# A decoder layer's kernel: the modulations ask for their weights one row of k tiles per portion, and VectorE makes one low part in two of the output projection's pairs

## The chip, the cores and the metric

The kernel runs on one core of one Trainium2 chip. The metric is the device time of one execution in microseconds (us). A core has TensorE (matmuls), VectorE, ScalarE and GpSimd (elementwise work), SyncE (here only issuing DMAs), and 16 DMA engines that all queues share. In the profile they are called PE, PEld (TensorE's weight loads), DVE, ACT, POOL and SP.

## What is computed

One layer of a decoder for 512 prompt tokens and 8 x 8 sample tokens, 576 columns in all, with D = 1024, in float32. Cut to what matters here:

```python
mod = jax.nn.silu(c) @ w_ada + b_ada          # 6 blocks of 1024, per sequence
sh1, sc1, g1, sh2, sc2, g2 = jnp.split(mod, 6, axis=-1)
h = _rmsnorm(x, norm1_g) * (1.0 + sc1) + sh1
b_gate, c_gate, xa, q, k, v, ga, gb = jnp.split(h @ w_in, cuts, axis=-1)
uc, new_conv = _causal_conv(c_gate * xa, conv_buf, conv_w)
ya = (b_gate * uc) @ w_conv_out
yb = attend(q, k, v, sinks) @ w_attn_out
x = x + g1 * ((jax.nn.sigmoid(ga) * ya + jax.nn.sigmoid(gb) * yb) @ w_mix_out)
h2 = _rmsnorm(x, norm2_g) * (1.0 + sc2) + sh2
# then the ConvFFN with w_up, w_down, its residual with g2, and a final RMSNorm
```

## The kernel before

**Products in three passes.** Every float32 operand is split into a high part (a copy to the matmul's type, made by ScalarE) and a low part (the operand minus the high part). A product is high x high + high x low + low x high, for each of the 8 tiles of 128 rows of k. Each operand needs its two parts before its matmuls.

**Pairs.** Most products are made two at a time (`pair_product`, line 382). Seven products of half the columns (288) replace eight: parts 1 to 7, of 12 matmuls each, with four sums of the weights ("A" holds a0 and a1, "B" holds s1 and b1, "C" holds s2 and s4, "D" holds s3) and sums of the operand. The four PSUM banks are X and W (from the pool `aux`, four banks) and Y and Z (from the pool `mm`, two tiles, so each pair takes over the banks of the pair before). Part 2 fills Y with s2, part 3 fills Z with s1. VectorE reads Y after part 2 (`u`, seen as `uv<-mm,p`); part 6 goes on in Y; VectorE reads it again after part 6 (`v`, the same form), and Z after part 7 (`uv<-mm,uv`). Only then can the next pair's parts 2 and 3 begin.

**The weights of a pair** are prepared during the pair before (`pair_weights`, line 326) from two raw tiles ra and rb of 128 x 8 x 128. `in_turn` (line 377) hangs the steps behind the parts: before part 1 "sums1 ah al", after part 2 "dh dl sums2", after part 3 "bh bl", after part 4 "ch cl". `sums1` and `sums2` are VectorE's sums, in place: `sums1` overwrites rb and makes the raw of "D", `sums2` overwrites ra (`raw<-raw,raw` and `raw<-raw` in the profile). A step with h is ScalarE's high part, one with l the low part. A low part is made in one of two ways:

```python
if name in adding:
    act.activation(lo, src, AF.Copy, scale=-1.0)
    pool.dma_start(lo, src, accum_op=ALU.add)
else:
    dve.tensor_tensor(out=lo, in0=src, in1=hi.bitcast(F32), op=ALU.subtract)
```

In the first way the transfer issued by GpSimd adds the raw weights, read from ra, to the negated copy. `al` reads ra, `sums2` writes it, so `sums2` waits for that transfer. The call's string names the weights that go the first way.

**Stages.** After the start-up, the keys, queries and values, and the convolution's products, come: four pairs for the gate B (`b_pair`), eight pairs for ga and gb (`sigmoid_pair`, "gate pairs"), two products and three pairs with `w_conv_out` (`out_pair`, lines 1424 to 1469; the projection's pairs), eight products with `w_attn_out` (lines 1497 to 1521), the products with `w_mix_out`, and the FFN. The weights of the first out pair are prepared in the last gate pair with `OUT_ADDING`; those of the second and third in the out pair before each (line 1459).

**The modulations as filler.** Two thirds of `mod` are made in between, by generators that run in portions: each step of a product over one k tile calls `tick()` (line 204), which adds a rate to a counter and runs a portion whenever it passes 1. A pair has 28 ticks, a product 8. `modulation(2048)` follows the attention's portions at `MOD_RATE`, during the B and gate pairs; `modulation(4096)` runs at the rate of line 1475 during the eight products with `w_attn_out`; what is left is run off by `drain()` behind them. One call makes 16 blocks of 128: for each k tile four loads of 128 x 512 of `w_ada` ("a row", tiles `ada`), a group of 16 small matmuls per two k tiles (`side_by_side`, line 1166, seen at L1171), then ScalarE copies the PSUM bank (`row`), TensorE transposes it (four transposes) and VectorE adds the bias.

**Queues and tiles.** TensorE, ScalarE and VectorE keep program order for what goes through the wrappers `pe`, `act` and `dve` (from line 1298 on); the row copy on ScalarE and the bias sum on VectorE do not go through them and are placed by the compiler's scheduler. SyncE's loads are placed by the scheduler too until line 1474, from where they keep program order. Tiles such as `ada`, `th`, `uv`, `mxh` and `st` share one pool of 57; a new one waits for the release of an old one. During the products with `w_attn_out` SyncE also loads, behind the fifth product, the state of the FFN (`st`, six tiles) and the residual x.

Of the kernel before, what the change touches and what calls it, by code (L numbers as in the profile page):

```python
# [30 lines left out]
CACHE_AT = 15, 16  # L31
UP_ADDING, FIRST_TICKS = "BD", 12
ATT_RATE, ADDING_FROM, B_PAIRS = 0.285, 3, ((0, 4), (1, 5), (2, 6), (3, 7))
B_ADDING, OUT_ADDING, MOD_RATE = "BD", "BCD", 12 / 190
EPS = 1e-6
NEG = -1e33
A_BUFS = 57
# [37 lines left out]
def step_kernel(ctx: ExitStack, tc: tile.TileContext, ins: dict, outs: list):  # L75
# [15 lines left out]
    def nm(s):  # L91
        cnt[0] += 1
        return f"{s}{cnt[0]}"

    def slot(s, dt=F32, shape=None):
        return ap_.tile(shape or [P, NT], dt, tag="a", name=nm(s))
# [4 lines left out]
    def aux():  # L101
        return pa.tile([P, 512], F32, tag="aux", name=nm("aux"))
# [49 lines left out]
    def load_w(src, nk):  # L152

        raw = wp.tile([P, nk, P], F32, tag="raw", name=nm("raw"), bufs=W_BUFS)
        sync.dma_start(raw, src)
        return raw
# [42 lines left out]
    def fill(gen, rate):  # L199
        filler[:] = [gen, rate, 0.0]  # L200
# [125 lines left out]
    def pair_weights(ra, rb, adding=""):  # L326


        c0, c1 = slice(0, 4), slice(4, 8)
        w = {}  # L330

        def add(out, x, y):
            dve.tensor_tensor(out=out, in0=x, in1=y, op=ALU.add)

        def tiles():
            return [wp.tile([P, NK, P], F32R, tag=t, name=nm(t), bufs=S_BUFS) for t in ("whi", "wlo")]

        def high(name, src, get):
            w[name] = hi, lo = get()
            act.activation(hi, src, AF.Copy)  # L340

        def low(name, src):
            hi, lo = w[name]
# [6 lines that stand above are left out]
        def s3_slots():  # L350
            return slot("wh", F32R, [P, 4, P]), slot("wl", F32R, [P, 4, P])

        def sums1():
            w["raw"] = slot("s3", shape=[P, 4, P])
            add(w["raw"], ra[:, c0], rb[:, c0])
            add(rb[:, c0], rb[:, c0], rb[:, c1])

        def sums2():
            add(ra[:, c0], ra[:, c0], rb[:, c0])
            add(ra[:, c1], ra[:, c1], ra[:, c0])  # L360

        def named(n0, n1, name):
            hi, lo = w[name]
            w[n0] = (lambda k: hi[:, k, :]), (lambda k: lo[:, k, :])
            if n1:
                w[n1] = (lambda k: hi[:, k + 4, :]), (lambda k: lo[:, k + 4, :])

        def one(name, src, get, n0, n1):
            return (lambda: (high(name, src(), get), named(n0, n1, name))), (lambda: low(name, src()))

        ah, al = one("A", lambda: ra, tiles, "a0", "a1")
        dh, dl = one("D", lambda: w["raw"], s3_slots, "s3", None)
        bh, bl = one("B", lambda: rb, tiles, "s1", "b1")
        ch, cl = one("C", lambda: ra, tiles, "s2", "s4")
        return w, dict(sums1=sums1, sums2=sums2, ah=ah, al=al, bh=bh, bl=bl, ch=ch, cl=cl, dh=dh, dl=dl)

    def in_turn(t):

        order = {0: "sums1 ah al", 2: "dh dl sums2", 3: "bh bl", 4: "ch cl"}
        return {at: (lambda names=names: [t[n]() for n in names.split()]) for at, names in order.items()}  # L380
# [46 lines left out]
    def kpm(w, m0, k0=0, nk=NK):  # L427
        return w[k0 * P : (k0 + nk) * P, m0 : m0 + P].rearrange("(k p) m -> p k m", p=P)
# [313 lines left out]
    for j in (2, 0, 1):  # L742
        t = slot("kT")
# [50 lines left out]
    for i in (3, 4):  # L794
# [3 lines left out]
        t = slot("kout", shape=[P, 256])  # L798
# [367 lines left out]
    def side_by_side(ps, ks, cols):  # L1166


        order = [(k, j) for k in reversed(ks) for j in (3, 0, 1, 2)]
        for n, (k, j) in enumerate(order):  # L1170
            done = nc.tensor.matmul(  # L1171
                ps[32 * j : 32 * j + 32, :], cT[:, k, :], cols[k][j],
                start=(k == 1), stop=(k == NK - 2),
            )
            if n:
                tc.keep_in_program_order(done)

    def modulation(c0):

        ps = aux()  # L1180
        cols = {}

        def rows(k):
            cols[k] = [slot("ada", shape=[P, 512]) for _ in range(4)]
            for j, t in enumerate(cols[k]):
                c = c0 + 512 * j
                sync.dma_start(t, ins["w_ada"][0, k * P : k * P + P, c : c + 512])

        rows(0)
        yield False  # L1190
        rows(1)
        yield False
        for k in range(0, NK, 2):
            yield False
            side_by_side(ps, (k, k + 1), cols)
            for kk in (k + 2, k + 3):
                if kk < NK:
                    rows(kk)
            yield False
        row = slot("row", shape=[P, 512])  # L1200
        nc.scalar.copy(row, ps)
        t = aux()
        yield False
        for cc in range(4):
            transpose(t[:, cc * P : cc * P + P], row[:, cc * P : cc * P + P], ident)
        b0 = c0 // P
        nc.vector.tensor_tensor(
            out=modT[:, b0 : b0 + 16, :].rearrange("p (j c) r -> p j c r", j=4),
            in0=t.rearrange("p (c j r) -> p j c r", c=4, j=4)[:, :, :, 0:9],
            in1=parT[:, b0 : b0 + 16]  # L1210
            .rearrange("p (j c) -> p j c", j=4)
            .unsqueeze(3)
            .to_broadcast([P, 4, 4, 9]),
            op=ALU.add,
        )
        yield False

    def modulations():
        yield from modulation(4096)
        yield True  # L1220

    def beside_conv():
        yield from attention()
        filler[1] = MOD_RATE
        yield from modulation(2048)
        yield True
# [7 lines left out]
    def conv_w(c0):  # L1234

        raw = load_w(kpm(w_in, c0), NK)
        if len(ys) < ADDING_FROM:
            return split_w(raw)
        w, low = w_split_adding(raw)
        low()  # L1240
        return w
# [6 lines left out]
    for m in range(NK):  # L1248
# [15 lines left out]
        w = conv_w(2048 + m * P)  # L1264
# [35 lines left out]
    def merged(*parts):  # L1300

        out = {}
        for at in range(8):
            fs = [p[at] for p in parts if at in p]
            if fs:
                out[at] = lambda fs=fs: [f() for f in fs]
        return out
# [74 lines left out]
    def part_o(n):  # L1382
        for k in range(len(o), n):
            o.append(split_slot(ot[k // 4][:, k % 4, :], "o"))
# [11 lines left out]
    def out_w(m, w):  # L1396

        w_next[m], low = w_split_adding(load_w(kpm(w, m * P), NK))
        low()

    def out_raws(n):
        return [load_w(kpm(wco, (2 * n + j) * P), NK) for j in range(2)]

    for n in range(len(gate_cols)):
        if n + 1 < len(gate_cols):
            steps = weights_for(n + len(B_PAIRS))
        else:
            drain()
            w, t = pair_weights(*out_raws(1), OUT_ADDING)
# [14 lines left out]
    def out_pair(m, w, steps):  # L1424
        def out(m, c):
            def done(x, y, op):
                dve.tensor_tensor(out=y, in0=x, in1=y, op=op)
                dve.tensor_tensor(out=sg[m][:, c], in0=y, in1=sg[m][:, c], op=ALU.mult)

            return done  # L1430

        a, b = slice(0, HT), slice(HT, NT)

        def a0(ps):
            dve.tensor_tensor(out=sg[m][:, a], in0=ps, in1=sg[m][:, a], op=ALU.mult)

        pair_product(w, made_g["op"], steps, a0, out(m, b), out(m + 1, a), out(m + 1, b))
# [18 lines left out]
    for n in (1, 2, 3):  # L1456
        parts = [{0: lambda: [op.n3() for op in ops]}] if n == 1 else []
        if n < 3:
            w, t = pair_weights(*out_raws(n + 1), "ABD")
            w_pair.append(w)  # L1460
            parts.append(in_turn(t))
        if n == 2:
            parts.append({5: lambda: part_o(1), 7: lambda: part_o(2)})
        if n == 3:
            parts.append({
                0: lambda: out_w(0, wao), 1: lambda: part_o(4), 3: lambda: out_w(4, wao),
                4: lambda: part_o(6), 6: lambda: part_o(7),
            })
        out_pair(2 * n, w_pair.pop(0), merged(*parts))
# [2 lines left out]
    ya = sg[:NK]  # L1472
    gb = sg[NK:]
    pinned.append(sync)
    fill(modulations(), 13 / 46)
    w_mix = ins["w_mix_out"][0]
    mixed, values, made_mix = [None] * NK, [None] * NK, {}
    ops, steps = [], {}
# [355 lines left out]
    def down_load(m, m0, m1):  # L1834
        return load_w(kpm(w_dn, m * P, m0, m1 - m0), m1 - m0)
# [106 lines left out]
    for m0, m1 in FCH:  # L1942
# [24 lines left out]
        if m1 < NF:  # L1967
# [3 lines left out]
            n = m1 - m0  # L1971
# [51 lines left out]
        n = m1 - m0  # L2023
# [4 lines left out]
        w = split_w(down_load(2, m0, m1))  # L2028
# [3 lines left out]
        for m in range(2, NK - LATE):  # L2032
            acc_m = product(w, fa)
            if m + 1 < NK - LATE:
                w = split_w(down_load(m + 1, m0, m1))
# [62 lines left out]
```

## Time and profile before

| | us |
|---|---|
| median of 3 runs | 984.25 (981.45 to 984.8) |
| profiled execution | 982.55 |
| its span, first to last instruction | 980.4 |
| TensorE busy | 962.9 |
| VectorE busy | 685.5 |
| ScalarE busy | 528.8 |

The profile is of one execution. Times in it count from the span's start. "x<-y" names the tile written and the tiles read; `mm` and `aux` are PSUM banks, `whi`/`wlo` the weights' parts, `raw` the raw weights. Busy times of TensorE include the overlap of pipelined matmuls. Rows of the chain of waits give a start, a length and what the time went to; a row of a timeline gives start, length, engine, line, operation, tiles and shape, and in brackets the idle time before it and who ended it. Line 114 is the wrapper's and says nothing of the place. A row of the view of stretches gives start:end, length, then busy us and count of PE, PEld, DVE, ACT and POOL, the granted clock, the DMA engines' share and GB/s.

### The profile page before, as it was taken

How to read it: one execution, taken by the hardware profiler on the slowest of the kernel's cores; microseconds unless marked ns; L12 is line 12 of the kernel's file. 1: busy time of each engine (PE TensorE's matmuls, PEld its weight loads, DVE VectorE, ACT ScalarE, POOL GpSimd, SP SyncE). 2: the span in 40 equal slices, each digit the busy share in tenths (PEclk: the TensorE clock that was granted, in tenths of full speed). 3: DMA queues.
4: the chain of work that ended last, by engine and by line, in shares of the span. 5: the costliest groups of instructions: out<-in, count | busy, mean ns of one | idle time of the engine just before them, and what ended most of it. 6: DMA issues, size and time to landing. Idle time of an engine off the chain costs nothing.

```text
span 980.4 us, 18958 instructions
## 1 busy us (share of the span) xinstructions
PE 962.9 (98%) x7408; PEld 926.5 (95%) x7408; DVE 685.5 (70%) x1334; ACT 528.8 (54%) x959; POOL 158.1 (16%) x349
## 2 busy tenths in 40 slices
PE   6999999999999999999999999999999999999997
PEld 5899999999997999999889999999999999999996
DVE  5736875674866778887578788785558874578753
ACT  5455667664753544685244478663347742256553
POOL 2222222011221100021000041220013310022120
PEclk9999999999999999999999999999999999999999
DMA  9984345474379523478972543682457762557502
GB/s 294 332 247 129 96 102 124 112 221 128 77 189 291 189 84 109 124 159 203 354 241 66 150 108 94 157 203 68 116 128 166 169 166 66 129 127 181 130 9 97
DMA packets 183851, 150.39 MB, mean 153 GB/s; under 512 B 8039, under 2 KB 161998, under 8 KB 183474
## 3 DMA queue, kind: packets, MB, share of 16 engines
q1 hardware_dynamic: 170242, 109.36, 36.7%
q0 software_dynamic: 13376, 39.57, 19.9%
q8 instruction: 58, 0.95, 0.4%
q14 instruction: 31, 0.25, 0.1%
q10 hardware_dynamic: 144, 0.26, 0.1%
HBM read 109.17 MB, written 7.35 MB: 119 GB/s over the span
## 4 chain that ended last, share of the span: by engine, by line
PE 90%; DVE 3%; DMA 3%; issue 2%; ACT 1%; POOL 0%; SPq 0%; POOLq 0%; DVEq 0%; ACTq 0%
PE mm L114 61%; PE aux L114 26%; DMA wlo<-raw 2%; PE aux L1171 2%; PE aux L1070 1%; DMA x<-in_x_prompt 1%; DVE gl L114 0%; DVE sg L114 0%; DVE tw L114 0%; ACT whi L114 0%; DVE cy L114 0%; DVE raw L114 0%; SPq L433 0%; DVE tl L114 0%; DVE wlo L114 0%
## 5 line engine op out<-in xcount | busy, mean ns | idle before, releaser
L114 ACT ACTIVATE whi<-raw 128x1024 fp32r<-128x1024 f32 (+2 forms) x173 | 177.5, 1035 | 106.7 <-PE mm L114 75.5
L114 DVE TENSOR_TENSOR wlo<-raw,whi 128x1024 fp32r<-128x1024 f32 (+2 forms) x126 | 149.3, 1188 | 43.5 <-ACT whi L114 41.8
L114 POOL DMA_DIRECT2D wlo<-raw x47 | 40.9, 870 | 399.6 <-ACT wlo L114 210.0
L114 PE MATMUL mm<-hh,whi 128*128 128x256 f32 (+1 forms) x448 | 103.2, 303 | 0.6 <-ACT hh L114 0.6
L114 PE MATMUL mm<-hh,wlo 128*128 128x256 f32 (+1 forms) x448 | 99.3, 294 | 0.0
L114 PE MATMUL mm<-hl,whi 128*128 128x256 f32 (+1 forms) x448 | 98.4, 295 | 0.1
L114 PE MATMUL mm<-th,wlo 128*128 128x288 f32 x280 | 82.8, 296 | 1.7 <-DMA wlo<-raw 1.7
L114 PE MATMUL mm<-th,whi 128*128 128x288 f32 x280 | 83.0, 296 | 1.4 <-DVE uv L114 1.4
L114 PEld LDWEIGHTS mm<-hh,whi 128*128 128x128 f32 x448 | 74.4, 188 | 9.8 <-issue 7.9
L114 PE MATMUL mm<-tl,whi 128*128 128x288 f32 x280 | 82.5, 295 | 0.0
L114 PEld LDWEIGHTS mm<-hh,wlo 128*128 128x128 f32 x448 | 75.8, 188 | 0.0
L114 PEld LDWEIGHTS mm<-hl,whi 128*128 128x128 f32 x448 | 75.2, 188 | 0.5 <-DVE hl L114 0.5
L114 PE MATMUL mm<-fh,whi 128*128 128x256 f32 (+1 forms) x304 | 65.3, 296 | 0.0
L114 PE MATMUL mm<-fh,wlo 128*128 128x256 f32 (+1 forms) x304 | 64.9, 294 | 0.0
L114 PE MATMUL mm<-fl,whi 128*128 128x256 f32 (+1 forms) x304 | 64.8, 295 | 0.0
L114 DVE SCALAR_TENSOR_TENSOR x<-mm,modT,x 128x512 f32<-128x512 f32 (+1 forms) x29 | 19.6, 677 | 62.0 <-PE mm L114 61.8
L114 PEld LDWEIGHTS mm<-th,whi 128*128 128x128 f32 x280 | 52.7, 188 | 2.1 <-DVE uv L114 1.1
L114 PEld LDWEIGHTS mm<-th,wlo 128*128 128x128 f32 x280 | 52.6, 188 | 1.9 <-DMA wlo<-raw 1.9
L114 PEld LDWEIGHTS mm<-tl,whi 128*128 128x128 f32 x280 | 52.6, 188 | 0.0
L114 PEld LDWEIGHTS mm<-fl,whi 128*128 128x128 f32 x304 | 51.0, 188 | 0.0
L114 PEld LDWEIGHTS mm<-fh,whi 128*128 128x128 f32 x304 | 50.8, 188 | 0.1
L114 PEld LDWEIGHTS mm<-fh,wlo 128*128 128x128 f32 x304 | 50.8, 188 | 0.0
(357 smaller groups left out, 2854.1 us busy)
## 6 DMA issues: line engine op xcount, KB each, us to landing
raw<-in_w_in SPq DMA_DIRECT2D x52, 512.0 KB, 4.7
wlo<-raw POOLq DMA_DIRECT2D x47, 512.0 KB, 4.8
raw<-in_w_up SPq DMA_DIRECT2D x44, 512.0 KB, 4.0
ada<-in_w_ada SPq DMA_DIRECT2D x64, 256.0 KB, 5.5
ad<-in_w_ada SPq DMA_DIRECT2D x32, 256.0 KB, 6.3
raw<-in_w_down SPq DMA_DIRECT2D x16, 512.0 KB, 4.0
wl<-s POOLq DMA_DIRECT2D x25, 256.0 KB, 4.6
raw<-in_w_conv_out SPq DMA_DIRECT2D x8, 512.0 KB, 4.4
```

What stands on the lines that cost most here:

```text
L114: done = getattr(self.engine, name)(*args, **kwargs)
L1070: done = nc.tensor.matmul(O[HALF[par], :256], vt(i - nkt + 1 + kt)[:, hd * 64 : hd * 64 + 64], pts[kt][:, par * 256 : par * 256 + 256], st ...
L1171: done = nc.tensor.matmul(ps[32 * j : 32 * j + 32, :], cT[:, k, :], cols[k][j], start=(k == 1), stop=(k == NK - 2),)
```

## The change

```diff
-B_ADDING, OUT_ADDING, MOD_RATE = "BD", "BCD", 12 / 190
+B_ADDING, OUT_ADDING, MOD_RATE = "BD", "BCD", 15 / 200
...
         for k in range(0, NK, 2):
             yield False
             side_by_side(ps, (k, k + 1), cols)
             for kk in (k + 2, k + 3):
                 if kk < NK:
                     rows(kk)
-            yield False
+                    yield False
         row = slot("row", shape=[P, 512])
         nc.scalar.copy(row, ps)
         t = aux()
...
         if n < 3:
-            w, t = pair_weights(*out_raws(n + 1), "ABD")
+            w, t = pair_weights(*out_raws(n + 1), B_ADDING)
             w_pair.append(w)
             parts.append(in_turn(t))
...
-    fill(modulations(), 13 / 46)
+    fill(modulations(), 15 / 50)
```

Two things change.

- In a modulation, the two rows asked for behind a group of matmuls come in two portions instead of one. Behind the last group, which asks for no row, no portion ends, so the row copy stands in the same portion as that group. A modulation has 14 portions and its end instead of 12 and its end, and both rates are raised.
- In the weights of the second and third out pair, the low part of "A" is made by VectorE's subtraction instead of by ScalarE's negated copy and an accumulating transfer. "B" and "D" go on by transfer, "C" by VectorE, as before.

## Prediction

> **What bounds the kernel now.** I read the page first: how busy TensorE is, and what the chain of work that ended last consists of.
>
> ```profile
> span 980.4 us, 18958 instructions
> PE 962.9 (98%) x7408; PEld 926.5 (95%) x7408; DVE 685.5 (70%) x1334; ACT 528.8 (54%) x959; POOL 158.1 (16%) x349
> PE 90%; DVE 3%; DMA 3%; issue 2%; ACT 1%; POOL 0%; SPq 0%; POOLq 0%; DVEq 0%; ACTq 0%
> ```
>
> TensorE is the bound. Nothing in the change adds or removes a matmul, so the change can pay or cost only where TensorE stands still. The view of TensorE's waits, taken from 60 us (after the start-up) to the end, lists all such places by what they waited for:
>
> ```profile
> PE mm L114 <- DMA wlo<-raw: 1.7, 1, 1.7
> PE mm L114 <- DVE uv L114: 1.4, 3, 0.8
> PE mm L114 <- ACT sq L114: 0.2, 1, 0.2
> ```
>
> That is all there is to win: one wait for an accumulating DMA and three for VectorE's tile `uv`. TensorE's timeline shows where they are (time, length, idle time before it and its releaser in brackets):
>
> ```profile
> 296.82 0.40 PE L114 MATMUL mm<-th,wlo 128*128 128x288 f32 x1 [1.70 <-DMA wlo<-raw]
> ...
> 441.96 0.40 PE L114 MATMUL mm<-th,whi 128*128 128x288 f32 x1 [0.30 <-DVE uv L114]
> ...
> 452.55 0.37 PE L114 MATMUL mm<-th,whi 128*128 128x288 f32 x1 [0.79 <-DVE uv L114]
> ...
> 454.67 0.40 PE L114 MATMUL mm<-th,whi 128*128 128x288 f32 x1 [0.29 <-DVE uv L114]
> ```
>
> The first is in the third `b_pair`; the other three are in the second and third `out_pair`, the projection's pairs that the change touches. Why is `uv` late there? The chain of waits through these pairs (start, length, what):
>
> ```profile
> 429.81 3.79 DMA wlo<-raw
> ...
> 435.49 0.70 DVE raw L114
> ...
> 440.25 7.14 DMA wlo<-raw
> ...
> 447.51 0.70 DVE raw L114
> ...
> 449.05 1.07 ACT whi L114
> ...
> 450.14 1.23 DVE wlo L114
> ...
> 452.03 0.38 DVE uv L114
> ```
>
> The DMAs issued at 429.81 and 440.25 are the low part of "A" (a0 and a1), ScalarE's negated copy with the raw weights added by a transfer. `sums2` (`raw<-raw,raw`) overwrites the tile that this transfer reads, so it waits for the landing; VectorE works in program order, so everything behind `sums2` waits too: `ch` on ScalarE, `cl`, and at last `uv`, which frees the PSUM bank that TensorE wants for the next pair. VectorE's own timeline shows it idle there, and ScalarE's (last row) idle behind it:
>
> ```profile
> 433.14 0.45 DVE L114 TENSOR_TENSOR uv<-mm,p 128x288 f32<-128x288 f32 x1
> 435.49 0.69 DVE L114 TENSOR_TENSOR raw<-raw,raw 128x512 f32<-128x512 f32 x1 [1.90 <-issue]
> ...
> 438.09 1.23 DVE L114 TENSOR_TENSOR wlo<-raw,whi 128x1024 fp32r<-128x1024 f32 x1 [0.82 <-ACT whi L114]
> ...
> 441.45 0.45 DVE L114 TENSOR_TENSOR uv<-mm,uv 128x288 f32<-128x288 f32 x1
> ...
> 443.64 0.45 DVE L114 TENSOR_TENSOR uv<-mm,p 128x288 f32<-128x288 f32 x1
> 447.51 0.69 DVE L114 TENSOR_TENSOR raw<-raw,raw 128x512 f32<-128x512 f32 x1 [3.42 <-DMA wlo<-raw]
> ...
> 449.05 1.06 ACT L114 ACTIVATE whi<-raw 128x1024 fp32r<-128x1024 f32 x1 [2.61 <-DVE raw L114]
> ```
>
> What these waits cost in all is read from the stretches of the three out pairs, beside a gate pair with the same matmuls and no wait (start:end, length, then busy time by engine):
>
> ```profile
> 380.91:392.05 11.14, 11.14 (x87) 11.14 (x86) 9.06 (x13) 5.66 (x10) 0.00 (x0) 1.00 0.34 96
> ...
> 427.07:438.23 11.16, 11.16 (x87) 11.16 (x86) 8.38 (x18) 7.11 (x12) 2.58 (x3) 1.00 0.89 191
> 438.23:450.01 11.78, 11.48 (x86) 11.19 (x85) 7.44 (x14) 6.44 (x9) 2.58 (x3) 1.00 1.01 223
> 450.01:462.73 12.72, 11.64 (x86) 11.21 (x85) 10.40 (x20) 10.13 (x16) 1.72 (x2) 1.00 0.71 166
> ```
>
> 0.02 + 0.64 + 1.58 = **2.24 us** over 11.14 each; the three brackets sum to 1.38, so a wait costs some 0.3 us beside its bracket. The granted clock is 1.00 throughout.
>
> **Part one: "A" made by VectorE in the out pairs.** Twice (weights for the second and the third out pair) it removes one ScalarE copy of 128x1024 (1.06 us, as `whi` at 449.05), one DMA issue on GpSimd, and one transfer of that size. It adds twice one VectorE subtraction of 128x1024: 1.23 us by the row at 438.09, placed after `sums1` and ahead of `u` (the `uv` at 433.14 and 443.64).
>
> First out pair. `al` runs where `uv` ran, from 433.14 to 434.36; `u` follows until 434.81; `sums2` is then free at once, since `ah` on ScalarE is long done: it starts at 434.85 instead of 435.49, 0.64 us earlier. The `ch`, `cl` and outputs behind it move by as much, and the `uv` at 441.45 to 440.81, ending at 441.26. TensorE wants that bank two of seven parts into its next pair, at 438.23 + 2/7 x 11.14 = 441.41, so its wait is gone. Second out pair. The start is 0.64 us earlier: `sums1` from 441.67, `al` 443.0 to 444.2, `u` to 444.65, `sums2` at 444.7 instead of 447.51, 2.8 us earlier. ScalarE is the next late one: it has `bh` and `bl` ahead of `ch`, and its idle time before 449.05 was 2.61 us, so `ch` comes 2.6 us earlier. `cl` and the `uv` at 452.03 follow by as much, to 449.4 and an end at 449.8; TensorE wants that bank at 450.01 − 0.64 + 1/7 x 11.14 = 450.96. The next bank, wanted a part later, comes free 2.6 us earlier too. Both remaining waits go. **−2.24 us.**
>
> Cover: in the first out pair `u` must have read its bank before TensorE's part 6, which begins at 427.07 + 5/7 x 11.16 = 435.04; `u` ends at 434.81, 0.2 us ahead. If that margin is gone, each tenth costs a tenth; at most both subtractions lie open, 2 x 1.23 = 2.46 us, which would make the sum +0.2. I take nothing for it, because the removed idle time (1.90 + 3.42 = 5.32 us) is twice what is added. The lighter transfers gain nothing by themselves: the low parts of "B" and "D" do not stop TensorE here.
>
> [...]
>
> **Part two: one row of k tiles per portion.** The four groups of matmuls, the 64 loads and their sizes stay. A row is four loads; I counted portions by the code's rates. In the first modulation (15/200 for 12/190), counted in ticks from the end of the attention, rows 0 and 1 are asked at 0 and 11 (before: 0 and 13), both still ahead of the weights of the third pair; rows 2 and 3 at 38 and 51 (both at 45); rows 6 and 7 at 118 and 131 (both at 108); the last group at 158 (140), its turn at 171 (172). This matters for the wait at 296.82. SyncE's timeline and the chain:
>
> ```profile
> 282.81 5.05 SPq L114 DMA_DIRECT2D ada<-in_w_ada  x8
> 289.88 7.30 SPq L114 DMA_DIRECT2D raw<-in_w_in  x2
> ...
> 287.94 8.84 DMA wlo<-raw
> ```
>
> Rows 0 and 1 already were two portions, and SyncE issued them in one run from 282.81. The low part of "B", issued at 287.94, shared the DMA engines with them and took 8.84 us. In the changed kernel these eight loads are asked in the same order, so I expect the same run and the same wait: **0**. Bounds: the wait goes, 1.70 + 0.3 = 2.0 us, or a burst moved by a few us makes it as much longer.
>
> In the second modulation (15/50 for 13/46; SyncE in program order) the groups move from ticks 15, 22, 29, 36 to 14, 24, 34, 44, and the rows from pairs at 15, 22, 29 to single ones at 14, 17, 24, 27, 34, 37. Loads are spread out and the attention projection's weights stand further ahead in the queue, but no wait is there to remove: **0**. The row copy now stands in the portion of the last group and the four transposes three ticks later; before they were seven apart. The rows for its price (the last two: time to landing of the attention projection's weights, and of the loads of `w_ada`):
>
> ```profile
> 483.51 7.00 SPq L114 DMA_DIRECT2D ada<-in_w_ada  x8
> 490.77 2.08 SPq L114 DMA_DIRECT2D raw<-in_w_attn_out  x2
> ...
> 482.42 1.85 PE aux L1171 x16
> ...
> 491.87 5.75 PE mm L114 x42
> ...
> 498.80 0.69 ACT L114 ACTIVATE th<-tw 128x576 fp32r<-128x576 f32 x1 [0.36 <-PE aux L1171]
> ...
> 499.72 0.57 ACT L1201 COPY row<-aux 128x512 f32<-128x512 f32 x1
> ...
> raw<-in_w_attn_out SPq DMA_DIRECT2D x8, 512.0 KB, 5.9
> ...
> DMA to landing us min/median/max: 2.8/5.5/7.5
> ```
>
> A tick is 5.75/7 = 0.82 us, three are 2.5 us, the copy is 0.57: hidden, with 1.9 us to spare, as long as ScalarE is free when the last group ends.
>
> **Sum.** −2.24 + 0 + 0. The profiled execution took 982.55 us (980.4 of span and 2.15 around it), so 980.3 on its own scale. The runs shown were 981.45, 984.25 and 984.8; with the profiled one the four average 983.26, and I put the forecast on that: **981.0 us**.
>
> **Rivals.** *Both waits go* (part one, and the burst at 282.81 is broken up). For: it is the only other wait of size, and SyncE isn't held to program order there. Against: the order of asking is the same. 983.3 − 2.2 − 2.0 = 979.1.
>
> *ScalarE holds the row copy* (slower). Place: the four transposes at tick 47, which TensorE takes in order. The last eight tiles of `w_ada` stay in the pool until tick 44, not 36; the row at 498.80 shows ScalarE already waiting for exactly such tiles. If rows 6 and 7 wait for the group at tick 34 (460.5 + 34 x 0.82 + 3 x 1.85 = 493.9 at its end), their eight loads take SyncE until 500.9, the weights behind them land at 506.8, and `whi` and the copy end at 508.4; the transposes are due at 460.5 + 47 x 0.82 + 4 x 1.85 = 506.4. Price 2.0 us; if those weights are issued only when the last load has landed (7.5 us after its issue at 500.0, so at 507.5 for 500.9), 8.6 us; middle 5.3. It decides from 2.24 on. 983.3 − 2.2 + 5.3 = 986.3. For: SyncE's order is fixed and row 7 is asked three ticks, not eleven, ahead of those weights. Against: at 483.51 SyncE ran ahead of its tick by a whole group.
>
> *VectorE takes the DMA's place*, the margin of 0.2 us being gone: +0.2, 983.4; the change then does not do what it seems to.
>
> **Chances.** Forecast 0.42, both waits 0.23, row copy 0.25, VectorE 0.10. A measurement tells about 0.3% (3 us) from no change. The forecast is 0.23% by itself, so 0.25 of it counts as no change and 0.17 as faster; both waits: 0.23 faster; row copy: 0.22 slower, 0.03 same; VectorE: 0.05 and 0.05. Faster 0.40, same 0.33, slower 0.27. The range goes from 979.1 less 1.6 (the scatter of the runs shown is 3.35) to 987.5, which takes in the row copy's middle and leaves its far end out; the forecast's own range is 979 to 983.
>
> **What would show it.** Right: the three out pairs at 11.14 to 11.2 us each, no wait for `uv`, `sums2` following `u` without idle time, two accumulating transfers fewer; 1.7 us of waiting for `wlo` left in the third `b_pair`. Wrong: TensorE waiting for `row` or for `ada`; a wait for `uv` at part 6 of the first out pair; a later landing of "B" or "D" in the `b_pair`s; or new waits after 530 us, where I expect none.

## The result and the profile after

| | us |
|---|---|
| before, median of 14 runs | 983.7 (981.45 to 988.13) |
| after, median of 14 runs | 987.69 (984.86 to 988.89) |
| ratio after / before, 95% interval | 1.0039 [1.0028, 1.0049] |
| span of the profiled execution, before and after | 980.4 and 985.7 |

The change made the kernel slower by 0.4%. The forecast was 981.0 us and its range ended at 987.5: the sign was wrong and the time lies outside the range.

The page of the changed kernel, its first line and the busy times:

```profile
span 985.7 us, 18944 instructions
PE 968.0 (98%) x7408; PEld 928.8 (94%) x7408; DVE 687.0 (70%) x1336; ACT 527.5 (54%) x957; POOL 156.7 (16%) x347
```

TensorE has the same 7408 records, and yet is busy 5.1 us longer than the 962.9 of before. So the loss is not standing still alone. The view of its waits, from 60 us on (line, what it waited for, us in all, times, longest):

```profile
PE aux L1171 <- DMA ada<-in_w_ada: 3.8, 1, 3.8
PE mm L114 <- ACT sq L114: 0.2, 1, 0.2
```

The three waits for `uv` are gone, and so is the wait for the low part of "B". In their place is one that before did not exist: the matmuls of a modulation (L1171) wait 3.8 us for a load of `w_ada`.

**The out pairs, where part one was meant to pay.** Stretches of the three out pairs after (start:end, length, busy us and count of PE, PEld, DVE, ACT, POOL, granted clock, DMA share, GB/s):

```profile
434.31:445.41 11.10, 11.10 (x87) 11.10 (x85) 10.21 (x19) 7.08 (x11) 1.70 (x2) 1.00 0.67 146
445.41:456.55 11.14, 11.14 (x87) 11.14 (x85) 10.06 (x19) 7.23 (x12) 1.70 (x2) 1.00 0.90 193
456.55:467.75 11.20, 11.20 (x87) 11.20 (x86) 8.15 (x17) 7.78 (x12) 1.70 (x2) 1.00 0.82 185
```

They sum to 33.44 us; before they took 11.16 + 11.78 + 12.72 = 35.66. TensorE is busy through all of each. VectorE's timeline in the first of them (start, length, operation, tiles):

```profile
440.44 1.22 DVE L114 TENSOR_TENSOR wlo<-raw,whi 128x1024 fp32r<-128x1024 f32 x1
441.57 0.45 DVE L114 TENSOR_TENSOR uv<-mm,p 128x288 f32<-128x288 f32 x1
441.94 0.68 DVE L114 TENSOR_TENSOR raw<-raw,raw 128x512 f32<-128x512 f32 x1
```

`al`, `u` and `sums2` follow one another with no idle time in brackets, where before `sums2` stood idle for 1.90 us ahead of it and in the next pair for 3.42. `u` ends at 442.02, and TensorE's part 6 begins at 434.31 + 5/7 x 11.10 = 442.24: the margin is 0.22 us.

**The first modulation, where the loss is.** The chain of waits after (start, length, what) shows what TensorE waited for:

```profile
287.41 10.11 DMA ada<-in_w_ada
297.52 0.14 issue
297.65 3.18 PE aux L1171 x10
```

The load was issued at 287.41 and landed at 297.52. TensorE's timeline after, the groups of that modulation (a group is 8 matmuls, not the 16 that the part on the kernel before names: each of them is two records in the trace, so a whole group is x16; idle time before it in brackets):

```profile
297.65 3.18 PE L1171 MATMUL aux<-ada,cT 128*32 128x512 f32 x10 [3.81 <-DMA ada<-in_w_ada]
...
302.55 1.05 PE L1171 MATMUL aux<-ada,cT 128*32 128x512 f32 x4
...
305.72 1.04 PE L1171 MATMUL aux<-ada,cT 128*32 128x512 f32 x2
...
322.81 1.92 PE L1171 MATMUL aux<-ada,cT 128*32 128x512 f32 x16
...
356.02 1.05 PE L1171 MATMUL aux<-ada,cT 128*32 128x512 f32 x4
360.76 1.91 PE L1171 MATMUL aux<-ada,cT 128*32 128x512 f32 x12
```

and the first two of them before:

```profile
301.54 1.92 PE L1171 MATMUL aux<-ada,cT 128*32 128x512 f32 x16
...
316.31 1.92 PE L1171 MATMUL aux<-ada,cT 128*32 128x512 f32 x16
```

The first group was whole at 301.54 and waited for nothing. After, it is split five, two and one, behind the ticks 4, 8 and 13 of the third pair, and its first five matmuls stand earlier in TensorE's order than their loads land. The last group is split two and six. A quarter of a group (x4) takes 1.05 us, more than half of what a whole one takes (1.92); a single matmul (x2) takes 1.04, and six (x12) 1.91. SyncE asked the first eight loads as before, in one run (the row of its timeline after):

```profile
283.40 4.69 SPq L114 DMA_DIRECT2D ada<-in_w_ada  x8
```

so the loads did not come later (283.40 for 282.81, the whole kernel standing 0.6 us later there); their reader came earlier.

**The balance.** Stretches of two pairs' length, from the fifth part of one pair to the fifth part of the next but one. The first stretch, from the second to the fourth `b_pair`, holds the third pair and the first group; the second holds the last group. Before:

```profile
286.74:313.03 26.29, 24.59 (x186) 22.75 (x185) 18.00 (x31) 10.95 (x15) 4.51 (x7) 1.00 1.03 280
340.28:365.01 24.73, 24.73 (x190) 23.13 (x189) 18.43 (x27) 11.83 (x19) 0.00 (x0) 1.00 0.30 86
```

and after, with the granted clock behind the wait in a short stretch of its own (second row):

```profile
287.32:319.13 31.81, 28.00 (x186) 23.24 (x185) 18.10 (x31) 11.18 (x15) 4.50 (x7) 0.95 0.85 225
297.00:300.25 3.25, 2.60 (x10) 0.59 (x10) 0.00 (x0) 0.00 (x0) 0.00 (x0) 0.50 1.05 209
346.38:372.30 25.92, 25.92 (x191) 23.31 (x189) 18.33 (x28) 11.78 (x19) 0.00 (x0) 1.00 0.32 93
```

The first stretch is 31.81 − 26.29 = 5.52 us longer. Idle time is 3.81 where it was 1.70: +2.11 (the wait for "B" lies within the new one). Busy time is 28.00 where it was 24.59: +3.41. Of these, 2.60 us ran at a granted clock of 0.50. There the group's records start in fours 0.82 and 0.86 us apart (297.65, 298.47, 299.33), and 0.43 us apart in a whole group at 1.00 (the one at 322.81). So about half of the 2.60, 1.3, is put down to the clock, an estimate; the other 2.1 are the two extra pieces of the group, some 1.05 each. The last group's split costs 25.92 − 24.73 = 1.19. In all +6.71, less 2.22 in the out pairs, is +4.5 of the 5.3 us between the spans; 0.6 of the rest was there already at 287 us, ahead of any difference described here, and is not explained. (The profiled execution of before, 982.55 us, is quicker than its median of 983.7, so the spans lie further apart than the medians, which differ by 4.0.)

### The profile page after: what moved, and what is told of

Same layout as the page of the kernel before. It is cut to its first block, busy times and chain, and to the rows that moved or that the text cites. A ratio compares the mean times of both kernels' runs of the same rounds, so it can differ in the third digit from the quotient of the medians.

```text
span 985.7 us, 18944 instructions
## 1 busy us (share of the span) xinstructions
PE 968.0 (98%) x7408; PEld 928.8 (94%) x7408; DVE 687.0 (70%) x1336; ACT 527.5 (54%) x957; POOL 156.7 (16%) x347
## 4 chain that ended last, share of the span: by engine, by line
PE 95%; DMA 2%; issue 1%; POOL 0%; DVE 0%; SPq 0%; ACT 0%; POOLq 0%; DVEq 0%; ACTq 0%
PE mm L114 64%; PE aux L114 28%; PE aux L1171 2%; PE aux L1070 1%; DMA ada<-in_w_ada 1%; DMA x<-in_x_prompt 1%; SPq L433 0%; ACT junk L114 0%; POOL r L114 0%; POOL xn L114 0%; DVE cs L440 0%; POOL rs L114 0%; DVE yo L114 0%; POOLq L2094 0%; DVEq L2094 0%
## 5 line engine op out<-in xcount | busy, mean ns | idle before, releaser
L114 DVE TENSOR_TENSOR wlo<-raw,whi 128x1024 fp32r<-128x1024 f32 (+2 forms) x128 | 151.7, 1188 | 46.4 <-ACT whi L114 45.0
```

The source lines that it names most:

```text
L114: done = getattr(self.engine, name)(*args, **kwargs)
```

## The experiments

All ratios are to the kernel before, run on the same chip in the same job. The experiments are called e1 to e11, as in the expectations. The theory is that of the group's place: the loss comes from where the first modulation's first group lands in TensorE's order. Its rivals: that row by row asking makes the loads late, that part one costs something, or that the second modulation does.

**Part one alone (e1), and part two alone (e2).** The kernel before with this edit, and the changed kernel with it undone:

```diff
-            w, t = pair_weights(*out_raws(n + 1), "ABD")
+            w, t = pair_weights(*out_raws(n + 1), B_ADDING)
```

> Part one alone: the kernel before, with only the low part of A of the second and third out pair made by VectorE. Theory (the loss comes from the first modulation's matmuls, not from this part): the three out pairs take 11.1 to 11.2 us each, 2.2 us less than before, and nothing else moves; against the kernel before 983.7 - 2.2 = 981.5, ratio 0.9977. Rival (VectorE's two added subtractions cost elsewhere): no gain or a loss, ratio 1.000 to 1.003.

> Part two alone: the changed kernel with A's low part by transfer again. Theory: the changed kernel's loss and 2.2 us more, 987.7 + 2.2 = 989.9, ratio to before 1.006; TensorE waits some 4 us for ada in the third b_pair. Rival (the two parts only hurt together, for instance by shared transfers): ratio within 1.002.

Part one alone: 980.8 us, ratio 0.9961 [0.9946, 0.9976], span 978.2 (before 980.4, so −2.2). By the ratio the gain is larger, some 3.8 us, and the expected 0.9977 lies just outside its interval. Part two alone: 990.14 us, ratio 1.0055 [1.0037, 1.0072]. TensorE's waits in the first:

```profile
PE mm L114 <- DMA wlo<-raw: 1.4, 1, 1.4
PE mm L114 <- ACT sq L114: 0.2, 1, 0.2
```

and in the second:

```profile
PE aux L1171 <- DMA ada<-in_w_ada: 4.9, 1, 4.9
PE mm L114 <- DVE uv L114: 0.6, 2, 0.3
```

Part one is a gain, part two the whole loss; the new wait comes with part two and the waits for `uv` go with part one.

**The group pinned to its place (e3).** The changed kernel, with the first matmul of each group in program order too:

```diff
-            if n:
-                tc.keep_in_program_order(done)
+            tc.keep_in_program_order(done)
```

> The changed kernel with every matmul of a modulation's group kept in program order, the first one too, so that the group stands whole at its own tick (13 of the third b_pair, not 4, 8 and 13). Theory (the place of the group is the loss): the wait for ada of 4.0 us, the slowed and split groups of the first modulation go (third b_pair and the later split group: some 8 us); the wait for the low part of B, 2.0 us, that the other wait had covered, may come back. 987.7 - 8.2 + 2.0 = 981.5, ratio to before 0.998; 0.996 if that wait stays away. Rival (the loads asked row by row land later, wherever the group stands): TensorE still waits for ada at the group, ratio 1.002 or more.

981.14 us, ratio 0.9968 [0.9956, 0.9979]. The wait for `ada` is gone, the one for "B" is back, and the groups are whole again; TensorE's waits and the first group's row:

```profile
PE mm L114 <- DMA wlo<-raw: 1.5, 1, 1.5
```

```profile
299.43 1.92 PE L1171 MATMUL aux<-ada,cT 128*32 128x512 f32 x16
```

So with the same portions, rates and loads the change gains about what part one alone gains: the ratios agree within their intervals, and the spans are 979.3 and 978.2. (The expected 0.998 lies just outside the interval; the gain is larger.) `side_by_side` (line 1166) keeps every matmul of a group in program order but the first. With the first one free, the compiler placed seven of the eight ahead of the group's tick; why the followers moved too is not shown. That freedom, with the new rate, is what cost the time.

**The first modulation alone (e4).** Part one, the first modulation as in the changed kernel, the second as before (two rows a portion, 13/46):

```diff
-    def modulation(c0):
+    def modulation(c0, single=True):
...
-                    yield False
+                    if single:
+                        yield False
+            if not single:
+                yield False
...
-         yield from modulation(4096)
+         yield from modulation(4096, False)
...
-    fill(modulations(), 15 / 50)
+    fill(modulations(), 13 / 46)
```

> Part one, and part two in the first modulation only; the second modulation asks for two rows per portion at 13/46 as before. Theory: the loss lies in the first modulation alone, so as the changed kernel: 987.7, ratio to before 1.004. Rival (the second modulation, its row copy or its loads, costs something): 1 to 3 us less than the changed kernel, ratio 1.001 to 1.003.

988.34 us, ratio 1.0043 [1.003, 1.0055], the changed kernel's loss, with a wait for `ada` of 3.6 us and the same pieces. The second modulation contributes nothing that can be measured.

**Rate or row by row?** First the changed kernel with the first modulation at the old rate (e5, the edit shown); then the kernel before with part one and the new rate in the first modulation, two rows to a portion (e6):

```diff
-B_ADDING, OUT_ADDING, MOD_RATE = "BD", "BCD", 15 / 200
+B_ADDING, OUT_ADDING, MOD_RATE = "BD", "BCD", 12 / 190
```

> Kernel: the changed one, single rows in both modulations, but the first modulation runs at the rate of before (12/190 for 15/200). Place theory: the loss hangs on where the first group of matmuls of the first modulation stands in TensorE's order, and the rate puts it there, not the asking row by row. At the old rate the first group stands whole at tick 20 of the third pair, as before; only the last group is split, two and six. So no wait for ada, the wait for the low part of B stays (1.4 to 2.0 us), and one split costs about 1.0: e1's 980.8 + 1.0 = 981.8 us, ratio about 0.998. Rival (asking row by row makes the loads late): a wait for ada of 3 us or more stays, 986 to 988 us, ratio 1.003.

> Kernel: the one before with part one, two rows to a portion as before, but the first modulation at 15/200. Place theory: TensorE's order has the first group split five, two, one at the same place as in the changed kernel, and the three others split six and two, six and two, two and six. So a wait for ada of 3.6 to 4 us in the third pair, and two splits more than in the changed kernel, at about 1.0 each: 987.7 + 1.9 = 989.6 us, ratio about 1.006. Rival (asking row by row is the cause): no wait for ada, 980.8 plus the splits (4 x 1.0) at most, 981 to 985 us, ratio below 1.001.

At the old rate: 982.39 us, ratio 0.9996 [0.9985, 1.0007]. Its wait and the first group, whole:

```profile
PE mm L114 <- DMA wlo<-raw: 1.7, 1, 1.7
```

```profile
301.69 1.92 PE L1171 MATMUL aux<-ada,cT 128*32 128x512 f32 x16
```

With the new rate and two rows: 989.13 us, ratio 1.0059 [1.0042, 1.0076], and

```profile
298.45 3.40 PE L1171 MATMUL aux<-ada,cT 128*32 128x512 f32 x10 [4.28 <-DMA ada<-in_w_ada]
303.69 1.05 PE L1171 MATMUL aux<-ada,cT 128*32 128x512 f32 x4
```

The wait follows the rate, not the asking row by row. At the old rate no gain is shown, the interval taking in 1, and the expected 0.998 lies just outside it. Its span of 980.3 is 2.1 above part one alone. The split of its last group accounts for about 1.2 and the longer wait for "B" for 0.3; the other 0.6 is open.

**The wait for "B" (e7).** Part one, and the low part of "B" for the third `b_pair` made by VectorE too:

```diff
-        w, t = pair_weights(*raws.pop(n), B_ADDING if n < len(B_PAIRS) - 1 else "")
+        w, t = pair_weights(*raws.pop(n), ("BD", "D", "BD")[n] if n < len(B_PAIRS) - 1 else "")
```

> Kernel: the one before with part one, and in the second b_pair the low part of B for the third pair is made by VectorE's subtraction too, not by the transfer. Theory: the wait for the low part of B in the third pair is a wait for that transfer alone, and VectorE has idle time in the second b_pair: the wait (1.6 us by the distance of TensorE's matmuls in e1) goes, 980.8 - 1.6 = 979.2 us, ratio about 0.9945, the least time so far. Rival (VectorE is itself too late there, or the transfers of w_ada then make D late): a wait for DVE wlo or DMA wlo of the same size in its place, 981 us, ratio 0.997 as e1.

979.1 us, the least time of all, ratio 0.996 [0.9946, 0.9974]; span 976.9. What is left of TensorE's waits from 60 us on:

```profile
PE mm L114 <- ACT sq L114: 0.2, 1, 0.2
```

The wait is gone and nothing took its place. The expected ratio of 0.9945 lies at the edge of its interval. The span is 1.3 us below that of part one alone, but the two ratios are alike, and the two kernels ran on different chips: that it beats both the kernel before and the changed one is shown, that it beats part one alone is not shown by the times.

**What the wait itself costs.** The pinned kernel with the rate raised, so that the group stands whole where the changed kernel has its first piece (e8); then with 18 transposes of the identity ahead of it to keep TensorE at work (e9):

```diff
-B_ADDING, OUT_ADDING, MOD_RATE = "BD", "BCD", 15 / 200
+B_ADDING, OUT_ADDING, MOD_RATE = "BD", "BCD", 0.1
```

```diff
+        if ks == (0, 1) and not warmed:
+            warmed.append(1)
+            for n in range(18):
+                done = nc.tensor.matmul(ps[:, :128], ident, ident, start=True, stop=True)
+                tc.keep_in_program_order(done)
```

> Kernel: the changed one with the matmuls of side_by_side all in program order (as e3), and the first modulation at 0.1 for 15/200, which puts the first group whole where the changed kernel has its first five instructions, at tick 4 of the third pair. Place theory: TensorE waits there for ada, 3.5 to 4.5 us, though nothing is split; and the rounds of matmuls behind the wait stand about 0.8 us apart where 0.43 is usual, as in the changed kernel, since TensorE had stood still. The third pair takes 11.14 + 4.0 + 1.75 + 1.2 to 1.6 = about 18.3 us. Rival (the slow rounds come from splitting, or from operands that trickle in): rounds of 0.43 here, about 17 us. Compare with e9 for what the pause does.

> Kernel: e8 with 18 transposes of the identity into the same bank ahead of the first group (about 0.2 us each, 3.6 us), which that group's first matmul overwrites: TensorE has work during most of the wait. If the slow rounds follow from TensorE's standing still, they are back to 0.43 us and the third pair takes 11.14 + 4.0 + 1.75 = about 17 us, 1.2 to 1.6 less than e8 although TensorE does more. Rival (the slow rounds come from the memory or the loads that land at that time): rounds of 0.8 us remain and the pair is as long as in e8, 18.3 us or more.

One run each, 982.2 and 983.46 us beside 983.86 of before. The first of them missed: TensorE waited only 2.8 us, and behind that the group ran at a granted clock of 1.00, so the stretch of a pair's length around it took 16.07 us, not 18.3. In the second the transposes outlasted the wait (17.19 us). They told one thing of the clock: this wait of 2.8 us did not bring it down.

```profile
296.89 1.92 PE L1171 MATMUL aux<-ada,cT 128*32 128x512 f32 x16 [2.82 <-DMA ada<-in_w_ada]
```

So the same pair of kernels at 0.12, where the group stands about 2 us earlier, near the end of the second `b_pair` (e10), with 15 transposes in the second (e11):

```diff
-B_ADDING, OUT_ADDING, MOD_RATE = "BD", "BCD", 0.1
+B_ADDING, OUT_ADDING, MOD_RATE = "BD", "BCD", 0.12
```

> Kernel: e8 with the first modulation at 0.12 for 0.1, so that the first group, whole, stands 15 matmuls (about 2 us) earlier in TensorE's order than in e8. Theory (the granted clock drops to 0.50 for some 3.4 us once TensorE has stood still for over 3 to 4 us, as in the changed kernel, e2, e4 and e6 with 3.7 to 5.1 us, and not in e8 with 3.0): the wait for ada is 4 to 5 us, the granted clock drops to 0.50 for about 3.4 us behind it, and the third pair takes 11.14 + 4.5 + 1.75 + 1.2 to 1.7 = about 18.8 us. Rival (the drop belongs to the split group, which all four kernels had that showed it): 1.00 throughout and 17.4 us.

> Kernel: e10 with 15 transposes of the identity ahead of the first group, about 3.4 us by e9, overwritten by that group. Theory (standing still brings the clock down): 1.00 throughout, a wait for ada of about 1 us left, the third pair at 11.14 + 4.5 + 1.75 = about 17.4 us, less than e10 though TensorE does more. Rival (the loads or the place bring it down): 0.50 for some 3.4 us as in e10 and 18.8 us.

985.91 and 984.95 us in one run each (before 982.37). Stretches of the first (the wait runs from 290.8 to 296.3): a pair's length around the group, from the fifth part of the second pair to the fifth of the third; then inside the wait; from 4.5 us behind its beginning on; and further on:

```profile
286.26:307.67 21.41, 15.87 (x102) 12.66 (x101) 8.96 (x15) 5.65 (x9) 2.74 (x4) 0.84 1.03 308
292.00:295.00 3.00, 0.00 (x0) 0.00 (x0) 0.00 (x0) 0.00 (x0) 0.04 (x1) 1.00 1.07 252
295.25:301.50 6.25, 5.17 (x22) 2.19 (x23) 0.46 (x1) 0.00 (x0) 0.00 (x0) 0.50 1.09 376
302.00:303.50 1.50, 1.50 (x13) 1.50 (x13) 1.47 (x3) 0.40 (x2) 0.09 (x1) 1.00 1.06 407
```

and of the second, a pair's length in the same place and the same stretch behind the transposes:

```profile
287.35:305.76 18.41, 16.60 (x132) 14.97 (x131) 8.88 (x15) 5.65 (x9) 2.74 (x4) 1.00 1.05 325
295.25:301.50 6.25, 4.46 (x35) 3.02 (x36) 1.83 (x4) 0.30 (x2) 0.53 (x1) 1.00 1.07 348
```

TensorE's wait for `ada` in the first and in the second:

```profile
PE aux L1171 <- DMA ada<-in_w_ada: 5.5, 1, 5.5
...
PE aux L1178 <- DMA ada<-in_w_ada: 1.8, 1, 1.8
```

The wait was 5.5 us, a us longer than expected, and the granted clock fell to 0.50 with a group that was not split: the pieces do not cause it. With work in front the clock stayed at 1.00, though the DMA engines were as busy (1.07 and 1.09) and a wait of 1.8 us was left, and the stretch was 3.0 us shorter in spite of 15 matmuls more. Both stretches are longer than expected: in both the wait was longer, and in the first the clock stayed at 0.50 for 6.8 us, not 3.4.

## Why the prediction was wrong

- **Part one: right, in size and in its steps.** −2.24 us was the term; the out pairs measured 33.44 for 35.66, −2.22, and part one alone took 2.2 off the span. `sums2` came free where it was put. (Before, its row in the first out pair named no releaser; the transfer issued at 429.81 took 5.6 us to land, until 435.4, just ahead of it.) It started without idle time, and the margin of 0.2 us between `u` and part 6 measured 0.22. VectorE did not become the bound: in the first out pair it was busy for 10.21 of 11.10 us, and TensorE did not wait for it in any of the three.
- **Part two, first modulation: the step that failed.** "In the changed kernel these eight loads are asked in the same order, so I expect the same run and the same wait: **0**." The first half held: one run of eight from 283.40, landed by 297.52. But I priced the loads alone and not their reader. A raised rate moves the groups of matmuls as well, and I worked out only the last group's tick. By ticks the first one went from 20 to 13 of the third pair, which would have been harmless: pinned there, it started at 299.43 and waited for nothing. It was not pinned, and its first piece stood behind the matmuls that end at 293.8, 3.7 us ahead of the landing. The term of 0 measured +6.7: 2.1 of waiting net of the wait for "B", 1.3 of work at a granted clock of 0.50 (an estimate), 2.1 and 1.2 of split groups. My bounds for this edit knew a later burst as the only loss.
- **The wait for "B": right by itself, hidden in the result.** It stays at 1.4 to 1.7 us with part one alone, with the group pinned and at the old rate, and vanishes in the changed kernel only because a longer wait lies over it. *Both waits go* happened on the surface, with the other sign.
- **Part two, second modulation: 0, right.** With the first modulation alone changed the loss was the same. The slower rival, ScalarE holding the row copy, did not happen: TensorE waits nowhere for `row`. Its price alone carried the range up to 987.5.
- **The signs.** "TensorE waiting for `row` or for `ada`" was named as what would show the forecast wrong, and the second of them did. There was no rival behind it, since it was not asked who may move a group.
- **The forecast as such** is what the pinned version takes: 981.14 us for 981.0.

## What to carry to other kernels

When filler work is re-paced, follow its readers on the bounding engine as well as its loads, and check for each whether program order holds it; here an instruction that was not held in program order was moved ahead of its data, and the group that was split paid for each extra piece, 1.05 to 1.19 us. A changed rate that meets no wait before can make one where nothing was listed. Look for a longer wait lying over a shorter one before counting the shorter as won, and cost a wait with the work behind it: here, with waits of 3.6 to 5.5 us, the granted clock was at 0.50 for 3.4 or 6.8 us.

## What the runs showed of the hardware

TensorE's granted clock fell to 0.50 in the runs with the longest waits for `ada`, and part of the loss came with the work behind, an estimated 1.3 us in the changed kernel. It stayed at 1.00 with idle times before the group of 1.8 us (e11) and 2.8 us (e8), and fell to 0.50 in all five runs with 3.6 us or more (3.6 in e4, 3.8 in the changed kernel, 4.3 in e6, 4.9 in e2 and 5.5 in e10). At 0.50 a whole group took 3.64 us (e10), at 1.00 1.92; the matmuls of 128x288 behind it started 0.24 us apart, and 0.13 from 301.97 on. With 3.6 us (e4) the clock fell only after TensorE had been at work again for 0.8 us, and in the changed kernel while it still waited. Stretches of 0.25 us in which the clock changes, in the changed kernel, in e4, and at both ends of the half rate in e10:

```profile
296.75:297.00 0.25, 0.00 (x0) 0.00 (x0) 0.00 (x0) 0.00 (x0) 0.09 (x1) 0.76 1.10 340
...
298.50:298.75 0.25, 0.25 (x5) 0.01 (x1) 0.00 (x0) 0.00 (x0) 0.00 (x0) 0.86 1.26 254
...
295.00:295.25 0.25, 0.00 (x0) 0.00 (x0) 0.00 (x0) 0.00 (x0) 0.00 (x0) 0.73 1.23 313
301.75:302.00 0.25, 0.25 (x3) 0.25 (x3) 0.25 (x2) 0.00 (x0) 0.25 (x1) 0.62 1.06 410
```

The clock was at 0.50 for 3.4 us in the changed kernel (296.9 to 300.3), for as long in e2, e4 and e6, and for 6.8, twice that, with the longest wait (295.1 to 301.9). It fell 3.0 us after TensorE's last matmul ended in the changed kernel (at 293.8), and 4.3 us after in e10 and 4.4 in e4. What sets the moment of the fall and the length is not shown, and between idle times of 2.8 and 3.6 us nothing was measured.

The other surprise is the price of splitting a group of small matmuls: 1.05 to 1.19 us for each extra piece, though no work is added. Most of it, by the trace, is room left empty. There the matmuls of a group (128*32) run four side by side: four records start within 0.02 us of each other, and the next four 0.43 us later. Each matmul of a group being two records, a whole group takes four such rounds (1.92 us). A piece of one or two matmuls takes two rounds (1.04 and 1.05), with one or two records in each, and one of five or six still takes four (1.91 for six). So each extra piece here adds two rounds, 2 x 0.43 = 0.86 us. Some 0.2 of the remaining 0.2 to 0.3 us stand at the two ends of a piece: it starts 0.22 us behind the matmul ahead of it (302.33 to 302.55), and the second matmul behind it starts 0.23 us after the first (303.54 to 303.77), where these matmuls otherwise start 0.13 us apart. No run isolates the cause.
